# Seven products instead of eight in more weight units of the down projections of a transformer block, and a wider spacing of such units in the output projections

## The chip, the core and the metric

The kernel runs on one core of a Trainium2 chip. The metric is the device time in microseconds of one execution. A core has a matrix engine (TensorE, PE in the profile, with its weight loads as PEld), VectorE (DVE), ScalarE (ACT), GpSimd (POOL) and SyncE (SP), which here starts nearly all transfers. Each engine takes its instructions in program order, and they wait for each other by semaphores.

## What is computed

One layer of a streaming encoder block in float32: 256 tokens, width D = 2048, a feed-forward width of 5632, 256 memory tokens.

```python
def swiglu(h, w_gate, w_up, w_down):
    return (jax.nn.silu(h @ w_gate) * (h @ w_up)) @ w_down

def reference(...):
    x = x + 0.5 * swiglu(rms_norm(x, ffn1_norm), ffn1_w_gate, ffn1_w_up, ffn1_w_down)
    h = rms_norm(x, mix_norm)
    u, q, k, v, g, a_lr = split(h @ w_in)          # one combined projection
    y = concatenate([pool_mixer(u, ...), gla_mixer(q, k, v, g, a_lr, ...)])
    x = x + y @ w_out
    x = x + mem_cross_attention(rms_norm(x, xattn_norm), rms_norm(mem, mem_norm), w_q, w_kv, w_o)
    x = x + 0.5 * swiglu(rms_norm(x, ffn2_norm), ffn2_w_gate, ffn2_w_up, ffn2_w_down)
    return rms_norm(x, final_norm)
```

## The kernel before

**Units.** All weights (some 418 MB are read from HBM) pass through the core once, in pieces of 1 MB, called units: a raw tile of 128x2048 float32, of which three are held. Two units ahead of its use (`AHEAD = 2`), a unit is split for products in fp32r: ACT copies the raw tile to its high part `wh` (L247), DVE subtracts to get the low part `wl` (L248); `wh` and `wl` have three buffers each. A product in float32 is then three matmuls, high by high, high by low and low by high (`products`, L325 to L330), each with a 128x128 tile of activations as the stationary operand and 512 columns of weights passing by. What goes between units (evictions, splits of activations, sums) is given to the stream as `st.op(f, n)`: after n more units. ACT's and DVE's order is held to the order of the program around the weights by `in_turn` and `among_weights`.

**Plain and seven.** A unit of a down or an output projection holds two k tiles of 128 and two column groups of 512 for both halves of 128 tokens: 8 products, 24 matmuls (L330). A unit "by sevens" (`seven`, matmuls in L456) does the same 2x2x2 block with Winograd's form of Strassen's scheme: 7 products, 21 matmuls. For that DVE forms sums T of the weight's quarters (L431), ACT and DVE split T (`wh` in L434, `wl` in L435) and three quarters of the raw tile (`xh` in L247, `xl` in L248). `Sums.make` forms the sums of the activations of one pair of k tiles, and writes over half of that pair in `ys`, so that from then on only units by sevens can read it. The scope of the output projections gives T and `xh` one pair of buffers to share and `xl` a single one.

**A block.** `block_s` multiplies into 1024 columns of x. The four whole products P2, P4, P3, P0 take two PSUM tiles of two banks; the parts P1, P6, P7, P5, which the units by sevens alone need, take two more. The pool has four such tiles in all. After the last unit by sevens, `combine` adds the parts up (ACT copy L512, DVE L513, L514, L517) and `merge` adds the two sums to x early (L707); at the block's end the residual adds the whole products (DVE, L695). A block without sevens is `block_t`.

**Who adds into x.** `into_x` does an output or a down projection as two halves of 1024 columns, for w_out, w_o and five of the six downs. Each feed-forward network is cut into three parts (`FF_PARTS`): two whole downs of 16 k tiles (8 units per half) and a rest of 12 k tiles (6 units per half). The second network's rest has a block of its own, `down_end`, and isn't touched here. Before, the whole downs and the output projections have pair 0 by sevens in the first half and pairs 0 and 4 in the second; the rest of the first network runs as `block_t`, without sevens.

**What follows the rest of the first network.** Each half of its result is folded: PE transposes 512 columns of x into one PSUM tile (`px`, L718), ACT and DVE split it into `xs` (L216, L217) for the next projection, and ACT takes the squares of x (L729). After the second half, the row factor of the norm is formed (an activation table load and a root on ACT, L195, and small steps on DVE), and w_in begins (`pa` tiles, L315). w_in's first two units of a block need the columns of the first half alone, its third and fourth those of the second.

The changed kernel's lines from `block_s` on are shifted: L454 for L456, L516 to L521 for L512 to L517, L699 for L695, L711 for L707, L722 for L718, L733 for L729.

Of the kernel before, what the change touches and what calls it, by code (L numbers as in the profile page):

```python
# [18 lines left out]
FF = 5632  # L19
# [71 lines left out]
def build(ctx, tc, I, out):  # L91
# [146 lines left out]
    def among_weights(f):  # L238


        scalar, vector = behind_weights(f)
        latest["vector"] = vector
        if scalar is not None:
            latest["scalar"] = scalar
# [127 lines left out]
    class Sums:  # L372
# [3 lines left out]
        def __init__(self, name, act, pairs, over):  # L376
            self.name, self.act, self.pairs, self.over = name, act, pairs, over
# [59 lines left out]
        ))  # L437
        return [[x.rearrange("p (b n) -> p b n", n=NB) for x in (th, tl, rh, rl)]], None

    def seven(banks, act, sums, g, fresh, ends, weights):  # L440
        th, tl, rh, rl = weights
        k0, k1, lo, hi = 2 * g, 2 * g + 1, slice(0, P), slice(P, S)
        a11, a12, a22 = ([act[:, k, p, t] for p in range(2)] for k, t in ((k0, lo), (k1, lo), (k1, hi)))
        s3, n1, n4, s2 = sums.parts(g)
        table = {
            "P1": (a11, rh[:, 0], rl[:, 0]), "P3": (n4, rh[:, 1], rl[:, 1]),
            "P2": (a12, rh[:, 2], rl[:, 2]), "P5": (n1, th[:, 0], tl[:, 0]),
            "P7": (s3, th[:, 1], tl[:, 1]), "P6": (s2, th[:, 2], tl[:, 2]),
            "P4": (a22, th[:, 3], tl[:, 3]),
        }  # L450
        order = ("P1", "P7", "P5", "P6", "P2", "P3", "P4") if "P1" in fresh else (
            "P1", "P2", "P3", "P7", "P5", "P6", "P4")
        for n in order:
            (a, b), wh, wl = table[n]  # L454
            for j, (x, w) in enumerate(((a, wh), (a, wl), (b, wh))):
                nc.tensor.matmul(  # L456
                    banks[n], x, w, start=n in fresh and j == 0, stop=n in ends and j == 2
                )

    def block_s(srcs, act, sums, order, evict, merge=None, sevens=None, late=0):  # L460

        sevens = [g for g in order if g in (sevens or sums.pairs)]
        held, seen = {"banks": {}}, set()

        def banks(*names):
            t = ptile(uid("pt"))
            for i, n in enumerate(names):
                held["banks"][n] = t[:, i]  # L470
            return t

        def open_whole():
            if "ps" not in held:
                c = banks("P2", "P4")
                held["ps"] = (banks("P3", "P0"), c)

        def open_parts():
            held["parts"] = (banks("P1", "P6"), banks("P7", "P5"))

        names = {(1, 0): "P2", (1, 1): "P4", (0, 0): "P3", (0, 1): "P0"}

        def unit_s(g):
            def fn(weights):
                if g == sevens[0]:
                    open_parts()
                open_whole()
                fresh = {f"P{i}" for i in range(1, 8)} - seen
                seen.update(fresh)
                ends = ("P1", "P5", "P6", "P7") if g == sevens[-1] else ()  # L490
                seven(held["banks"], act, sums, g, fresh, ends, weights)
            return fn

        def unit_p(g):
            def fn(wh, wl):
                open_whole()
                wh, wl = (w.rearrange("p (k j n) -> p k j n", j=2, n=NB) for w in (wh, wl))
                for j in (1, 0):
                    for h in range(2):
                        n = names[j, h]  # L500
                        for kk in range(2):
                            products(held["banks"][n], act, 2 * g + kk, h, wh[:, kk, j],
                                     wl[:, kk, j], n not in seen and kk == 0,
                                     g == order[-1] and kk == 1)
                        seen.add(n)
            return fn

        def combine():

            e = held["e"] = scope["pool"].tile([P, 4, NB], F32, tag="sg", name=uid("sg"), bufs=2)  # L510
            a, b = held["parts"]
            nc.scalar.copy(e[:, 0], a[:, 0])  # L512
            nc.vector.tensor_tensor(out=e[:, 3], in0=a[:, 1], in1=e[:, 0], op=ALU.add)  # L513
            nc.vector.tensor_tensor(  # L514
                out=e[:, 1:3], in0=b, in1=e[:, 3:4].to_broadcast([P, 2, NB]), op=ALU.add
            )  # L516
            last = nc.vector.tensor_tensor(out=e[:, 3], in0=b[:, 1], in1=e[:, 1], op=ALU.add)  # L517
            if merge is not None:
                merge(e[:, 2:4], e[:, 0:2])
            return None, last  # L520

        def join(j):
            if merge is not None:
                evict(j, held["ps"][j])
                return
            e = held["e"][:, 0:2] if j else held["e"][:, 2:4]
            among_weights(lambda: (None, nc.vector.tensor_tensor(  # L527
                out=e, in0=held["ps"][j], in1=e, op=ALU.add if j else ALU.subtract
            )))
            evict(j, e)  # L530

        for g in order:
            if g in sevens:
                st.unit(srcs[g], unit_s(g), split_seven)
                if g == sevens[-1]:
                    st.op(combine if merge else lambda: among_weights(combine), late)
            else:
                st.unit(srcs[g], unit_p(g))
        for j in (1, 0):
            st.op(lambda j=j: join(j))  # L540
# [150 lines left out]
    def residual(scale, b, last=1):  # L691

        def evict(j, ps):
            x = x_cols((2 * b + j) * NB, NB)
            nc.vector.scalar_tensor_tensor(  # L695
                out=x, in0=ps, scalar=scale, in1=x, op0=ALU.mult, op1=ALU.add
            )
            if j == last:
                store_x(b)  # L699
        return evict  # L700

    def early_parts(scale, b):

        def merge(minus, plus):
            for j, e, s in ((1, plus, scale), (0, minus, -scale)):
                x = x_cols((2 * b + j) * NB, NB)
                nc.vector.scalar_tensor_tensor(  # L707
                    out=x, in0=e, scalar=s, in1=x, op0=ALU.mult, op1=ALU.add
                )
        return merge  # L710

    def fold(c, gain):
# [14 lines left out]
        for h in range(2):  # L727
            q = tmp.tile([P, NB], F32, tag="j", name=uid("j"))
            nc.scalar.activation(q, x[:, h], AF.Square, accum_out=ss[:, h, c : c + 1])  # L729


    Y_PAIRS, Y_ORDER, Y_SEVEN = (0, 4), ((1, 2, 3, 4, 0, 5, 6, 7), (1, 2, 0, 3, 4, 5, 6, 7)), ((0,), (0, 4))
    y_sums = Sums("ye", ys, Y_PAIRS, True)  # L733

    def make_y_sums(first=2):
        for g, after in zip(Y_PAIRS, (first, 4)):
            st.op(lambda g=g: among_weights(lambda: y_sums.make(g)), after)

    def into_x(w, act, scale, gain=None, k0=0, nk=KT, spread_too=True, src=None,
               sums=None):  # L740

        for b in range(2):
            st.op(lambda b=b: fetch_x(b, src), 2)
            cols = wwide(w, b * 2 * NB, k0, nk)
            if sums is None:
                block_t(cols, act, residual(scale, b))
            else:
                block_s(cols, act, sums, Y_ORDER[b], residual(scale, b, 0), early_parts(scale, b),
                        Y_SEVEN[b])
            if gain is not None:  # L750
                for j in range(2):
                    st.op(lambda c=2 * b + j: fold(c, gain), 1)
        if gain is not None:
            st.op(lambda: finish_norm(4, spread_too), 2)
            if spread_too:
                st.op(spread_norm, 3)
# [7 lines left out]
    def ffn(wg, wu, wd, down, amid=None):  # L764
# [40 lines left out]
        for lo, n in FF_PARTS:  # L805
# [18 lines left out]
            if n % 2:  # L824
# [5 lines left out]
                        ev_up(0, c)  # L830
                block_s(wtwo(wu, wg, (lo + n - 1) * NB), xs, x_sums, ORDER, both)
                st.op(lambda n=n: turn(gate[0], 4 * (n - 1)), 1)
            if whole:
                make_y_sums()
            down(wd, 4 * lo, 4 * n, lo + n == FF // NB, y_sums if whole else None)

    st.op(lambda: spare_transposes(12))
    st.op(lambda: turn_gains(0, G_MIX))
# [11 lines left out]
    st.op(more_gains, 14)  # L850
    st.op(lambda: turn_gains(G_MIX, G_END), 35)

    def down_first(wd, k0, nk, last, sums):
        into_x(wd, ys, 0.5, G_MIX if last else None, k0, nk, src=None if k0 else I["x"][0],
               sums=sums)

    ffn(I["ffn1_w_gate"][0], I["ffn1_w_up"][0], I["ffn1_w_down"][0], down_first,
        amid_first)
# [321 lines left out]
        for j in range(4):  # L1180
            split_scaled(xs, 4 * c + j, v[:, j, :], gcol(G_MEM + 4 * c + j))

    make_y_sums(1)
    into_x(I["w_out"][0], ys, 1.0, G_X, sums=y_sums)
    st.op(mem_in, 2)
    for c in range(4):
        st.op(lambda c=c: behind_weights(lambda: mem_squares(2 * c, 2 * c + 2)), c + 3)
# [75 lines left out]
    for h in range(H):  # L1263
# [2 lines left out]
        st.op(lambda h=h: probs(h), 3)  # L1266
        block_b(wblock(w_kv, D + h * NB), xs, ev_V)
        st.op(lambda h=h: values(h), 1)
    make_y_sums(0)
    into_x(w_o, ys, 1.0, G_FFN2, spread_too=False, sums=y_sums)  # L1270
    st.op(close_scope, 1)
    st.op(open_scope("s_ffn2"), 1)

# [4 lines left out]
        fin["gB"] = scope["pool"].tile([P, D], F32, tag="T", name="gB")  # L1278
        nc.sync.dma_start(fin["gB"], I["final_norm"].partition_broadcast(P))

    def down_last(wd, k0, nk, last, sums):
        if last:
            down_end(wd, k0, nk)
        else:
            into_x(wd, ys, 0.5, None, k0, nk, sums=sums)

    def down_end(wd, k0, nk):

# [193 lines left out]
```

## Time and profile before

| | |
|---|---|
| time, median of 3 runs | 2101.9 us (2101.67 to 2102.31) |
| profiled execution: its own time | 2101.99 us |
| profiled execution: span of its instructions | 2100.2 us |
| mean granted TensorE clock | 0.998 |
| PE busy | 2085.5 us (99%), 9916 matmuls |
| DVE busy | 1704.1 us (81%) |
| ACT busy | 1108.3 us (53%) |
| DMA | 435.95 MB, mean 208 GB/s |

The span goes from the first to the last instruction of the profiled execution; its own time is somewhat longer. A row of the timeline or of a group names the engine, the line of the kernel, the operation, `out<-in` by the names of the tiles (without buffer numbers) and the shape; in brackets stands how long the engine had been idle before it and what ended that. Matmuls are pipelined: one that is listed with 0.39 us can be followed by the next after 0.23.

### The profile page before, as it was taken

To read this page: it belongs to the slowest core of one execution; us is meant where nothing else is said; L and a number is where in the kernel's file an instruction comes from. 1 tells how busy PE (TensorE), PEld (TensorE's weight loads), DVE (VectorE), ACT (ScalarE), POOL (GpSimd) and SP (SyncE) were. 2 spreads that over 40 slices of the span, in tenths; PEclk is the share of its full clock that TensorE was granted. 3 is DMA by queue.
4 is the path that set the end of the run, shared out by engine and by line. 5 is a ranking of instruction groups with operands and counts; after the bars stand their busy time and mean duration, and the time that the engine had idled before them with its cause. 6 is when DMAs were issued, how large, how long until landed. Compare 5 with 4: busy or idle time off the path is not lost.

```text
span 2100.2 us, 24513 instructions
## 1 busy us (share of the span) xinstructions
PE 2085.5 (99%) x9916; PEld 1743.5 (83%) x9916; DVE 1704.1 (81%) x1537; ACT 1108.3 (53%) x1084; POOL 14.1 (1%) x41
## 2 busy tenths in 40 slices
PE   9999999999999999999999999999999999999998
PEld 7878888888888888888888888888888888888886
DVE  7998899988996677688765555779998999989974
ACT  7654455644554555364645444466554556545544
POOL 0000000000000000000000000000000000000001
PEclk9999999999999999999999999999999999999999
DMA  7656666566656555467755555656577665676673
GB/s 262 202 198 221 239 220 210 190 238 234 210 198 254 195 180 195 152 195 246 253 180 166 172 165 168 213 198 223 181 238 226 226 202 189 222 243 216 206 257 118
DMA packets 143610, 435.95 MB, mean 208 GB/s; under 512 B 9861, under 2 KB 13545, under 8 KB 143113
## 3 DMA queue, kind: packets, MB, share of 16 engines
q1 hardware_dynamic: 143464, 434.38, 61.4%
q8 instruction: 78, 1.28, 0.2%
q14 instruction: 36, 0.29, 0.0%
q10 hardware_dynamic: 32, 0.01, 0.0%
HBM read 417.58 MB, written 16.78 MB: 207 GB/s over the span
## 4 chain that ended last, share of the span: by engine, by line
PE 93%; DVE 4%; issue 1%; ACT 1%; DMA 0%; SPq 0%; DVEq 0%
PE pt L330 45%; PE pt L456 20%; PE pa L315 15%; PE pb L330 6%; PE pe L330 3%; DVE T L431 1%; PE ph L797 1%; DVE wl L248 1%; DVE wl L435 1%; DVE xl L248 1%; PE pl L1217 1%; PE pv L1252 1%; PE px L718 0%; ACT wh L247 0%; DVE sg L527 0%
## 5 line engine op out<-in xcount | busy, mean ns | idle before, releaser
L248 DVE TENSOR_TENSOR wl<-raw,wh 128x2048 fp32r<-128x2048 f32 (+2 forms) x284 | 637.9, 2251 | 268.4 <-ACT wh L247 267.3
L247 ACT CAST wh<-raw 128x2048 fp32r<-128x2048 f32 (+2 forms) x284 | 533.1, 1881 | 396.5 <-PE pt L330 170.1
L330 PE MATMUL pt<-wh,xs 128*128 128x512 f32 x1536 | 494.8, 390 | 0.4 <-ACT xs L216 0.4
L330 PE MATMUL pt<-wh,ys 128*128 128x512 f32 x1440 | 449.0, 390 | 0.0
L434 ACT CAST wh<-T 128x1024 fp32r<-128x1024 f32 x196 | 206.0, 1053 | 307.2 <-DVE T L431 281.1
L330 PEld LDWEIGHTS pt<-wh,xs 128*128 128x128 f32 x1536 | 287.5, 188 | 59.5 <-ACT xs L216 0.6
L330 PEld LDWEIGHTS pt<-wh,ys 128*128 128x128 f32 x1440 | 269.9, 188 | 56.0 <-ACT wh L247 0.4
L315 PE MATMUL pa<-xs,wh 128*128 128x512 f32 x896 | 315.9, 397 | 0.0
L330 PE MATMUL pt<-wl,xs 128*128 128x512 f32 x768 | 299.8, 390 | 0.0
L330 PE MATMUL pt<-wl,ys 128*128 128x512 f32 x720 | 280.5, 390 | 0.0
L315 PE MATMUL pa<-xs,wl 128*128 128x256 f32 x896 | 248.3, 281 | 0.0
L435 DVE TENSOR_TENSOR wl<-T,wh 128x2048 fp32r<-128x2048 f32 x98 | 223.9, 2285 | 1.5 <-ACT wh L434 1.3
L315 PEld LDWEIGHTS pa<-xs,wh 128*128 128x128 f32 x896 | 167.6, 188 | 38.1 <-issue 0.3
L248 DVE TENSOR_TENSOR xl<-raw,xh 128x1536 fp32r<-128x1536 f32 x98 | 171.7, 1752 | 12.9 <-ACT xh L247 12.9
L315 PEld LDWEIGHTS pa<-xs,wl 128*128 128x128 f32 x896 | 169.1, 189 | 1.7 <-issue 0.2
L330 PEld LDWEIGHTS pt<-wl,xs 128*128 128x128 f32 x768 | 144.2, 188 | 30.0 <-DVE wl L248 0.2
L330 PEld LDWEIGHTS pt<-wl,ys 128*128 128x128 f32 x720 | 135.2, 188 | 28.0
L247 ACT CAST xh<-raw 128x1536 fp32r<-128x1536 f32 x98 | 145.0, 1479 | 21.9 <-PE pt L456 16.5
L431 DVE TENSOR_TENSOR T<-T,raw 128x512 f32<-128x512 f32 x196 | 135.4, 691 | 5.6
L456 PE MATMUL pt<-wh,xs 128*128 128x512 f32 x320 | 124.6, 389 | 0.0
L456 PE MATMUL pt<-wh,xe 128*128 128x512 f32 x320 | 123.9, 389 | 0.0
L456 PE MATMUL pt<-xh,xs 128*128 128x512 f32 x320 | 120.0, 392 | 1.7 <-DVE sg L527 1.6
(236 smaller groups left out, 2341.7 us busy)
## 6 DMA issues: line engine op xcount, KB each, us to landing
raw<-in_ffn_w_down SPq DMA_DIRECT2D x88, 1024.0 KB, 5.4
raw<-in_ffn_w_up SPq DMA_DIRECT2D x80, 1024.0 KB, 5.0
raw<-in_ffn_w_gate SPq DMA_DIRECT2D x77, 1024.0 KB, 5.0
raw<-in_w_in SPq DMA_DIRECT2D x32, 1024.0 KB, 5.2
raw<-in_xattn_w_kv SPq DMA_DIRECT2D x32, 1024.0 KB, 5.3
raw<-in_w_out SPq DMA_DIRECT2D x16, 1024.0 KB, 5.6
raw<-in_xattn_w_q SPq DMA_DIRECT2D x16, 1024.0 KB, 6.0
raw<-in_xattn_w_o SPq DMA_DIRECT2D x16, 1024.0 KB, 5.6
```

The lines of the kernel that those rows point to most:

```text
L247: in_turn("scalar", lambda: nc.scalar.copy(hi, src))
L248: in_turn("vector", lambda: nc.vector.tensor_tensor(out=lo, in0=src, in1=f32(hi), op=ALU.subtract))
L315: nc.tensor.matmul(o, w, x, start=k == 0 and i == 0, stop=last and i == 1)
L330: nc.tensor.matmul(ps, a, w, start=first and i == 0, stop=last and i == 2)
L431: in_turn("vector", lambda: nc.vector.tensor_tensor(out=o, in0=a, in1=b, op=ALU.add))
L434: in_turn("scalar", lambda: nc.scalar.copy(th[:, c], t[:, c]))
L435: in_turn("vector", lambda: nc.vector.tensor_tensor(out=tl, in0=t, in1=f32(th), op=ALU.subtract))
L456: nc.tensor.matmul(banks[n], x, w, start=n in fresh and j == 0, stop=n in ends and j == 2)
L797: nc.tensor.transpose(v[:, i, h * P : (h + 1) * P], g[:, h, i * P : (i + 1) * P], ident)
L1217: nc.tensor.matmul(ps[:, t, :M], ys[:, 4 * h + d, a, tok], xa["K"][:, d, b, :], start=i == 0, stop=i == 11,)
L1252: nc.tensor.matmul(ps[:, d, :S], xa["V"][:, m, a, col], xa["PT"][:, m, b, :], start=i == 0, stop=i == 5,)
```

## The change

Where units by sevens stand, and how many there are, is now given for each kind of projection by a small class `IntoX`: pairs, when the sums of activations are made, the order of the units in both halves, and which pairs run by sevens.

- Whole downs (`WHOLE`): pairs 0 and 4 by sevens in both halves, where the first half had only pair 0; pair 4 moves to the seventh place of the first half, and its sums are made a unit later.
- Output projections (`OUTPUT`): the same pairs as before; in the second half two plain units stand between the two by sevens, where there was one.
- The last down of the first network (`REST`): pair 0 by sevens in the first half, pairs 0 and 2 in the second, three units in all, through `block_s` and with sums of the activations, where it had none.
- The order of the seven products in a unit that is not its block's first one by sevens becomes P1, P2, P4, P3, P5, P6, P7 (was P1, P2, P3, P7, P5, P6, P4) in these projections.

```diff
+                if "P1" in fresh:
+                    order = ("P1", "P7", "P5", "P6", "P2", "P3", "P4")
+                elif merge:
+                    order = ("P1", "P2", "P4", "P3", "P5", "P6", "P7")
+                else:
+                    order = ("P1", "P2", "P3", "P7", "P5", "P6", "P4")
...
-    Y_PAIRS, Y_ORDER, Y_SEVEN = (0, 4), ((1, 2, 3, 4, 0, 5, 6, 7), (1, 2, 0, 3, 4, 5, 6, 7)), ((0,), (0, 4))
-    y_sums = Sums("ye", ys, Y_PAIRS, True)
-
-    def make_y_sums(first=2):
-        for g, after in zip(Y_PAIRS, (first, 4)):
-            st.op(lambda g=g: among_weights(lambda: y_sums.make(g)), after)
...
+    class IntoX:
+        def __init__(self, pairs, after, orders, sevens):
+            self.sums = Sums("ye", ys, pairs, True)
+            self.after, self.orders, self.sevens = after, orders, sevens
+
+        def make_sums(self, after=None):
+            for g, n in zip(self.sums.pairs, after or self.after):
+                st.op(lambda g=g: among_weights(lambda: self.sums.make(g)), n)
+
+    WHOLE = IntoX((0, 4), (2, 5), ((1, 2, 3, 5, 0, 6, 4, 7), (1, 2, 0, 3, 4, 5, 6, 7)),
+                  ((0, 4), (0, 4)))
+    OUTPUT = IntoX((0, 4), (0, 4), ((1, 2, 3, 4, 0, 5, 6, 7), (1, 2, 0, 3, 5, 4, 6, 7)),
+                   ((0,), (0, 4)))
+    REST = IntoX((0, 2), (2, 4), ((1, 2, 3, 4, 0, 5), (1, 3, 0, 4, 2, 5)), ((0,), (0, 2)))
...
-            if sums is None:
-                block_t(cols, act, residual(scale, b))
-            else:
-                block_s(cols, act, sums, Y_ORDER[b], residual(scale, b, 0), early_parts(scale, b),
-                        Y_SEVEN[b])
+            block_s(cols, act, way.sums, way.orders[b], residual(scale, b, 0),
+                    early_parts(scale, b), way.sevens[b])
...
-            if whole:
-                make_y_sums()
-            down(wd, 4 * lo, 4 * n, lo + n == FF // NB, y_sums if whole else None)
+            down(wd, 4 * lo, 4 * n, lo + n == FF // NB, WHOLE if whole else REST)
...
-    make_y_sums(1)
-    into_x(I["w_out"][0], ys, 1.0, G_X, sums=y_sums)
+    OUTPUT.make_sums((1, 4))
+    into_x(I["w_out"][0], ys, 1.0, G_X)
...
-    make_y_sums(0)
-    into_x(w_o, ys, 1.0, G_FFN2, spread_too=False, sums=y_sums)
+    OUTPUT.make_sums()
+    into_x(w_o, ys, 1.0, G_FFN2, spread_too=False)
```

More of the change, by code (lines that the diff above doesn't have):

```diff
@@ L438, in split_seven, with seven @@
         return [[x.rearrange("p (b n) -> p b n", n=NB) for x in (th, tl, rh, rl)]], None
-    def seven(banks, act, sums, g, fresh, ends, weights):
+    def seven(banks, act, sums, g, fresh, ends, weights, order):
         th, tl, rh, rl = weights
@@ L450, in seven @@
         }
-        order = ("P1", "P7", "P5", "P6", "P2", "P3", "P4") if "P1" in fresh else (
-            "P1", "P2", "P3", "P7", "P5", "P6", "P4")
         for n in order:
@@ L490, in fn @@
                 ends = ("P1", "P5", "P6", "P7") if g == sevens[-1] else ()
-                seven(held["banks"], act, sums, g, fresh, ends, weights)
+                if "P1" in fresh:
[4 more added lines that the diff above has]
+                    order = ("P1", "P2", "P3", "P7", "P5", "P6", "P4")
+                seven(held["banks"], act, sums, g, fresh, ends, weights, order)
             return fn
@@ L729, in fold, with into_x @@
             nc.scalar.activation(q, x[:, h], AF.Square, accum_out=ss[:, h, c : c + 1])
-    Y_PAIRS, Y_ORDER, Y_SEVEN = (0, 4), ((1, 2, 3, 4, 0, 5, 6, 7), (1, 2, 0, 3, 4, 5, 6, 7)), ((0,), (0, 4))
-    y_sums = Sums("ye", ys, Y_PAIRS, True)
-    def make_y_sums(first=2):
-        for g, after in zip(Y_PAIRS, (first, 4)):
-            st.op(lambda g=g: among_weights(lambda: y_sums.make(g)), after)
-    def into_x(w, act, scale, gain=None, k0=0, nk=KT, spread_too=True, src=None,
-               sums=None):
+    class IntoX:
[10 more added lines that the diff above has]
+    REST = IntoX((0, 2), (2, 4), ((1, 2, 3, 4, 0, 5), (1, 3, 0, 4, 2, 5)), ((0,), (0, 2)))
+    def into_x(w, act, scale, gain=None, k0=0, nk=KT, spread_too=True, src=None, way=OUTPUT):
         for b in range(2):
@@ L851, in build, with down_first @@
     st.op(lambda: turn_gains(G_MIX, G_END), 35)
-    def down_first(wd, k0, nk, last, sums):
+    def down_first(wd, k0, nk, last, way):
+        way.make_sums()
         into_x(wd, ys, 0.5, G_MIX if last else None, k0, nk, src=None if k0 else I["x"][0],
-               sums=sums)
+               way=way)
     ffn(I["ffn1_w_gate"][0], I["ffn1_w_up"][0], I["ffn1_w_down"][0], down_first,
@@ L1279, in last_gain, with down_last @@
         nc.sync.dma_start(fin["gB"], I["final_norm"].partition_broadcast(P))
-    def down_last(wd, k0, nk, last, sums):
+    def down_last(wd, k0, nk, last, way):
         if last:
@@ L1284, in down_last @@
         else:
-            into_x(wd, ys, 0.5, None, k0, nk, sums=sums)
+            way.make_sums()
+            into_x(wd, ys, 0.5, None, k0, nk, way=way)
     def down_end(wd, k0, nk):
```

## The prediction

> **What bounds the kernel now.** I read the busy times and the slices first, then the list of what TensorE waited for, then the chain that ended last.
>
> ```profile
> PE 2085.5 (99%) x9916; PEld 1743.5 (83%) x9916; DVE 1704.1 (81%) x1537; ACT 1108.3 (53%) x1084; POOL 14.1 (1%) x41
> ...
> PEclk9999999999999999999999999999999999999999
> ```
>
> TensorE (PE) is busy 2085.5 of 2100.2 us, at full clock in every slice. A product removed is therefore time removed, as long as its operands still come in time. VectorE (DVE) at 81% is the engine whose queue can be late.
>
> ```profile
> PE pt L456 <- DVE sg L527: 1.6, 4, 1.0
> PE pwarm L186 <- POOL ident masks.py:199: 1.4, 1, 1.4
> PE px L654 <- DMA x<-in_x: 0.9, 1, 0.9
> PE pt L456 <- DVE xl L248: 0.7, 2, 0.3
> ```
>
> Columns: total wait in us, how often, the longest. There is almost nothing to win from waits (the four rows make 4.6 us), and much to lose: any new wait of PE counts in full, because no later wait could swallow it.
>
> ```profile
> 204.35 4.76 PE pt L456 x21
> 209.11 27.20 PE pt L330 x120
> ```
>
> These two pieces of the chain (start, us, line, count) lie in the first whole down. 27.20/120 = 4.76/21 = 0.2267 us per 128x512 product in both kinds of unit: a plain 1 MB unit of 24 products takes 5.44 us of PE, one by seven products (21) takes 4.76.
>
> **The change, part by part.** All against the profiled execution (2101.99 us; its span 2100.2 and 1.8 around it), which lies 0.09 above the median 2101.9.
>
> *Products.* Each of the four whole downs takes one more unit by sevens (pair 4 in the first half), the last down of the first network takes three: 7 x 3 = 21 products less. 21 x 0.2267 = **-4.76 us**, if PE waits for nothing new.
>
> *Output products.* In the second half of w_out and w_o the two units by sevens have one plain unit between them; they get two.
>
> ```profile
> 980.45 1.48 ACT L247 CAST xh<-raw 128x1536 fp32r<-128x1536 f32 x1 [5.41 <-PE pt L456]
> ...
> 981.96 1.76 DVE L248 TENSOR_TENSOR xl<-raw,xh 128x1536 fp32r<-128x1536 f32 x1 [6.41 <-ACT xh L247]
> ...
> 982.97 0.46 PE L456 MATMUL pt<-wh,ys 128*128 128x512 f32 x1
> 983.77 0.50 PE L456 MATMUL pt<-xl,ys 128*128 128x512 f32 x1 [0.34 <-DVE xl L248]
> ...
> 986.54 0.39 PE L456 MATMUL pt<-wh,ys 128*128 128x512 f32 x1
> ...
> 1368.94 0.46 PE L456 MATMUL pt<-wh,ys 128*128 128x512 f32 x1
> 1369.74 0.50 PE L456 MATMUL pt<-xl,ys 128*128 128x512 f32 x1 [0.34 <-DVE xl L248]
> ```
>
> Timeline rows: start, us, engine, line, and in brackets the idle time before with its end. ACT's copy xh of the second such unit waits 5.41 us until PE has read out the first one's; xl follows it on DVE, and PE arrives before xl is done. From 982.97 to 986.54 there are 11 products: 3.57 - 11 x 0.2267 = 1.08 us lost, and at 1368.94 the same wait stands again. The plain unit put between moves PE's need back by 5.44 us; the 1.08 of lateness and the 2.29 of that unit's own subtraction (the row at 253.25, below) leave 2.1 us. So both waits go: **-2.1 us**. Bounds: 0 (the copy is still late) and -2.2.
>
> *Whole downs.* In the first half the second seven now stands one plain unit before the half's end, so the combine of its parts (four DVE steps and two merges into x) meets the residual and the next unit's preparation at the boundary. The same steps stood in the trace already in the second half, in this order:
>
> ```profile
> 251.25 0.69 DVE L513 TENSOR_TENSOR sg<-pt,sg 128x512 f32<-128x512 f32 x1 [0.42 <-ACT sg L512]
> 251.97 1.23 DVE L514 TENSOR_TENSOR sg<-pt,sg 128x1024 f32<-128x1024 f32 x1
> 253.25 2.29 DVE L248 TENSOR_TENSOR wl<-raw,wh 128x2048 fp32r<-128x2048 f32 x1
> 255.46 1.22 DVE L431 TENSOR_TENSOR T<-raw 128x1024 f32<-128x1024 f32 x1
> 256.60 0.68 DVE L517 TENSOR_TENSOR sg<-pt,sg 128x512 f32<-128x512 f32 x1
> 257.20 1.22 DVE L707 SCALAR_TENSOR_TENSOR x<-sg,x 128x1024 f32<-128x1024 f32 x1
> 258.33 0.69 DVE L431 TENSOR_TENSOR T<-T,raw 128x512 f32<-128x512 f32 x1
> 258.93 1.22 DVE L707 SCALAR_TENSOR_TENSOR x<-sg,x 128x1024 f32<-128x1024 f32 x1
> 260.07 0.68 DVE L431 TENSOR_TENSOR T<-T,raw 128x512 f32<-128x512 f32 x1
> 260.67 1.75 DVE L248 TENSOR_TENSOR xl<-raw,xh 128x1536 fp32r<-128x1536 f32 x1
> 262.34 2.28 DVE L435 TENSOR_TENSOR wl<-T,wh 128x2048 fp32r<-128x2048 f32 x1
> ```
>
> Count from the end of part P6 (after it ACT's copy of 0.6 us). By the start-to-start steps of these rows DVE takes 0.72 + 1.28 (sums of parts) + 2.21 (wl of the next plain unit) + 1.14 (T) + 0.60 + 1.13 (merge) + 0.60 (T) + 1.14 (merge) + 1.13 (residual, priced as a merge, same shape) + 0.60 (T) + 1.67 (xl) + 1.13 (residual) + 2.29 (wl of T): 0.66 + 15.64 = 16.3 us. PE has 76 products to issue between P6's last and the first that reads this wl: 76 x 0.2267 = 17.2, less 0.16 by which a product ends after its slot (0.39 against 0.2267): 17.07. **The margin is about 0.75 us**, at four places; the next plain units' wl have 1.0 to 1.2. So I cost it at nothing, with DVE's queue as the thin cover. If DVE comes x us later than this, each place costs x - 0.75. No transfer is moved by more than a unit, and none is near its need.
>
> *Last down of the first network.* Here PE waited for nothing before. In the changed program's queues three things follow from the two buffers of PSUM that the fold of x's first half holds: the parts P1, P5, P6, P7 of both sevens of the second half can't begin until DVE has split the folded columns, and their 24 products stand at the very end of the down. Until then those two units (128 and 130) keep two of the three wh and wl buffers.
>
> ```profile
> 690.54 1.91 ACT L247 CAST wh<-raw 128x2048 fp32r<-128x2048 f32 x1
> ...
> 692.49 2.29 DVE L248 TENSOR_TENSOR wl<-raw,wh 128x2048 fp32r<-128x2048 f32 x1 [1.45 <-ACT wh L247]
> ...
> 711.02 2.51 DVE L695 SCALAR_TENSOR_TENSOR x<-pt,x 128x1024 f32<-128x1024 f32 x2
> ...
> 712.10 0.39 PE L315 MATMUL pa<-xs,wh 128*128 128x512 f32 x1
> ...
> 714.12 0.62 ACT L729 ACTIVATE j<-x 128x512 f32<-128x512 f32 x1
> ...
> 727.68 4.50 DVE L248 TENSOR_TENSOR wl<-raw,wh 128x2048 fp32r<-128x2048 f32 x2 [1.31 <-ACT wh L247]
> ...
> 731.74 0.28 PE L315 MATMUL pa<-xs,wl 128*128 128x256 f32 x1
> ```
>
> (a) Unit 131 has only the buffer of 129. Its cast can start when 129's last product has ended; cast and subtraction take 4.24 us (690.54 to 694.78), with the 0.2 of product end and semaphore 4.45. PE has 11 products ahead of the first that needs the wl (nine of seven 130 and the first of 131, by the queue): 2.49. New wait **2.0 us**.
> (b) The first tile of w_in takes the PSUM buffer of P1 and P6, which is free when DVE's first sum of parts has read it. In DVE's queue the wl of unit 133 stands ahead of that sum, and its cast waits for unit 128's buffer, read last 12 products before the down's end. 0.2 + 1.95 (cast) + 2.2 (wl) + 0.69 (sum) - 12 x 0.2267 = **2.3 us**.
> (c) The residual is now behind everything. From the last product's slot DVE does that sum (start at 1.62, 0.60), a wl (2.20), the sums (1.28, 0.60), two merges (1.13 each) and two residuals (1.13, 1.22): 10.9 us. In the trace it was done 1.4 us after (711.02 + 2.51 against 712.10). Squares, rsqrt, the splits of the folded columns 2 and 3 and the wl of w_in's fourth unit hang on it. Before, the squares began 2.0 us after w_in's first product (714.12, 712.10). Now w_in's first product comes 2.3 after the slot and the squares 10.9: 8.6, so the chain runs 6.6 us later against PE. The fourth unit's wl was done at 729.97 (727.68, and 2.29 for the first of the two) and needed at 731.74: 1.8 of cover. 6.6 - 1.8 = **4.8 us**, split over waits for the third unit's xs (about 1.5) and the fourth's wh and wl (the rest).
> Sum of (a) to (c): **+9.1 us**. Bounds: 4.3 if the chain of (c) is hidden whole (the trace hid 1.8 of it, no row hides more); 12 if, besides, the first half's buffers cost as (a) does and DVE loses another 1 us in (c). I take 9.1, since each step has a row of the same operation and shape.
>
> Sum: -4.76 - 2.1 + 0 + 9.1 = **+2.2 us: 2104.2 for the profiled execution, 2104.1 by the median**. About 0.2% (4.2 us) is what a measurement of this kernel tells from no change, so it comes out within that.
>
> **Rivals.**
> 1. *Faster: products count, waits don't come.* 2101.9 - 4.76 - 2.1 = 2095.0; with (a) and (b) alone 2099.3. For it: PE's share of 99% and only 4.6 us of waits in the whole trace, though DVE's queue held the same steps in other downs. Against: in the whole downs no fold holds PSUM, and there is no rsqrt behind the residual; here the queue order leaves PE nothing else to issue. 0.15.
> 2. *Slower: DVE is late at the boundary of the whole downs.* It decides from 0.75 us of lateness, at four places. With 1.5 us each costs 0.75: 3.0, 2107.0. For it: the margin is a sum of thirteen steps, and ACT and DVE hand xh, wh and T to each other there. Against: in the rows above these steps ran back to back. 0.10.
> 3. *The output products' wait stays* (the change doesn't do what it says): the xh buffer is still asked for too early or the next unit's xh takes the wait. 2106.1. Against: 2.1 us of spare. 0.07.
> 4. *The last down costs more:* its first half, with a seven and the combine there, loses what (a) loses, and (c) 1 us more: 2107.0 to 2108. 0.08.
> 5. *The clock falls.* This row is the last 10.2 us of the span (columns: busy us and count of PE, PEld, DVE, ACT, POOL; then the granted clock):
>
> ```profile
> 2090.00:2100.20 10.20, 0.59 (x3) 0.17 (x1) 3.94 (x11) 3.38 (x9) 0.99 (x1) 0.66 0.56 202
> ```
>
> With PE nearly idle the clock granted is 0.66 there. The waits of (b) and (c) come within 25 us of each other; if they brought one such stretch, 0.34 x 10.20 = 3.5 us more: 2107.5. Against: none of them is longer than about 2.3 us, and the waits listed at the head (1.4 us the longest) were passed at full clock. 0.05.
> The Trainium skill (TensorE: Matmul & The Clock Gate, "The HAM clock gate" and "HAM oscillation") says that the array's clock halves after an idle window of some 3.4 us, and warns of PE gaps longer than that. By that rule a wait of 2.3 us alone leaves the clock, and the sum stays; the last row's 0.66 agrees with a fall after a few us of idleness, and no run here shows the threshold.
> The skill speaks for (a) and (b) too: Trainium Kernel Development and Optimization, "Best Practices", says that consistent bubbles can mean that SBUF or PSUM ran out.
>
> **How the numbers follow.** The forecast has 0.55; its own range, with 7 to 11 us for the last down, is 2102 to 2106. Rival 1 lies below 2097.7 with 0.12 and above it with 0.03. Of the rest, rivals 2, 4 and 5 are over 2106.1 with 0.20 together, rival 3 with half of its 0.07, and the forecast's upper edge with 0.03. That makes faster 0.12, same 0.61, slower 0.27. The range of 8 in 10 goes from 2098.5 (most of rival 1 outside) to 2108.
>
> **What would show it.** Right: in the changed kernel's waits of PE, the rows for xl at 983 and 1370 are gone; about 2 us appear in the second half of the last down for wh and wl; then, in the 30 us after it, 2.3 for the sum of parts and 4 to 5 for xs and wh; the residual ends some 11 us after the down's last product; the whole downs are 0.68 us shorter each with no wait. Wrong: no PE wait between 690 and 740 (rival 1), waits for T's wl in the whole downs (rival 2), or a granted clock under 1 after the last down (rival 5).

## The result and the profile after

The changed kernel takes 2107.74 us (median of 8 runs, 2106.69 to 2108.51) against 2101.99 (8 runs, 2101.32 to 2102.38): 5.75 us slower, ratio 1.0027, 95% interval 1.0016 to 1.0038. The profiled execution has 2108.27 us and a span of 2106.5, 6.3 more than before.

The first row of the profile's page, and then the waits of PE in the changed kernel (total us, times, longest):

```profile
PE 2085.8 (99%) x9895; PEld 1743.1 (83%) x9895; DVE 1743.9 (83%) x1589; ACT 1120.0 (53%) x1104; POOL 13.1 (1%) x41
```

```profile
PE pa L315 <- ACT wh L247: 2.6, 2, 1.6
PE pa L315 <- DVE sg L517: 2.2, 1, 2.2
PE pt L330 <- DVE wl L248: 2.2, 2, 1.1
PE pt L454 <- DVE sg L531: 1.6, 4, 1.0
PE pwarm L186 <- POOL ident masks.py:199: 1.4, 1, 1.4
PE pt L330 <- ACT wh L247: 0.4, 1, 0.4
```

PE has 21 matmuls less (the prediction calls each matmul of 128x512 a product, and so does this part) and is still busy for 0.3 us more. The rows for xl are gone, as forecast for the output projections. New are waits of `pa` (w_in) for the first sum of parts (2.2) and for wh (2.6), and of `pt` for wl (2.2) and wh (0.4): one wl of 1.1 in the last down, and one that was not forecast.

The timeline around the end of the last down, PE first, then DVE and ACT:

```profile
713.22 0.50 PE L315 MATMUL pa<-xs,wh 128*128 128x512 f32 x1 [2.21 <-DVE sg L517]
...
714.85 0.63 PE L315 MATMUL pa<-xs,wh 128*128 128x512 f32 x1
715.28 0.41 PE L315 MATMUL pa<-xs,wl 128*128 128x256 f32 x1
715.49 0.63 PE L315 MATMUL pa<-xs,wh 128*128 128x512 f32 x1
...
717.33 0.40 PE L315 MATMUL pa<-xs,wh 128*128 128x512 f32 x1
...
735.62 0.73 PE L315 MATMUL pa<-xs,wh 128*128 128x512 f32 x2 [1.55 <-ACT wh L247]
737.42 1.01 PE L315 MATMUL pa<-xs,wh 128*128 128x512 f32 x2 [1.07 <-ACT wh L247]
...
710.27 2.29 DVE L248 TENSOR_TENSOR wl<-raw,wh 128x2048 fp32r<-128x2048 f32 x1 [0.39 <-ACT wh L247]
712.48 0.68 DVE L517 TENSOR_TENSOR sg<-pt,sg 128x512 f32<-128x512 f32 x1
713.08 2.28 DVE L248 TENSOR_TENSOR wl<-raw,wh 128x2048 fp32r<-128x2048 f32 x1
...
719.41 2.35 DVE L699 SCALAR_TENSOR_TENSOR x<-pt,x 128x1024 f32<-128x1024 f32 x2
...
721.79 0.63 ACT L733 ACTIVATE j<-x 128x512 f32<-128x512 f32 x1 [8.85 <-DVE x L699]
```

The last product of the down has its slot at 710.62 to 710.85. PE then waits for DVE's first sum, which stands behind a wl (the rows at 710.27 and 712.48), as read from the queue. The residual ends at 721.76, 10.9 us after that slot (forecast 10.9), and the squares begin right behind.

What was not in the sum is between 713.8 and 717.2: a pair of products, wh and wl, takes 0.64 us (714.85 to 715.49) where it takes 0.35 elsewhere. The stretches of the changed kernel (busy us and count of PE, PEld, DVE, ACT, POOL; granted clock; DMA):

```profile
715.00:717.00 2.00, 2.00 (x8) 1.71 (x7) 1.97 (x3) 0.00 (x0) 0.00 (x0) 0.50 1.04 400
719.00:721.00 2.00, 2.00 (x13) 1.77 (x12) 2.00 (x3) 0.00 (x0) 0.32 (x1) 1.00 0.52 200
735.00:740.00 5.00, 3.32 (x11) 2.46 (x12) 4.41 (x2) 4.17 (x3) 0.00 (x0) 0.77 0.17 27
```

TensorE ran at half clock for some 3.4 us after the 2.2 us wait, and again from 737.7 to 741.1 after 1.55 and 1.07 (the ends are read from slices of half a microsecond). In 3.4 us at half clock PE does 1.7 us less of its work; how much of that reaches the time is told with the last down, below.

The stages, by the starts of their first and last products in the traces of both (us):

| stage | before | after | difference |
|---|---|---|---|
| four whole downs together | 346.3 | 343.6 | -2.7 |
| last down of the first network | 67.76 | 67.85 | +0.1 |
| from its end to w_out (w_in, pool, GLA) | 204.69 | 213.56 | +8.9 |
| w_out | 87.73 | 86.57 | -1.2 |
| from its end to w_o | 295.34 | 296.37 | +1.0 |
| w_o | 90.62 | 89.47 | -1.15 |
| from its end to the second network's first down | 170.48 | 171.80 | +1.3 |

They make +6.25, the whole difference of the spans. Each of the three parts of the change now has its own lines: the whole downs gained what was forecast, the output projections gained 2.3 and gave 2.3 back right behind, and the last down costs 9.0 net.

### The profile page after: what moved, and what is told of

Read it like the earlier page. It is cut to its first block, busy times and chain, and to the rows that moved or that the text cites. A ratio compares the mean times of both kernels' runs of the same rounds, so it can differ in the third digit from the quotient of the medians.

```text
span 2106.5 us, 24569 instructions
## 1 busy us (share of the span) xinstructions
PE 2085.8 (99%) x9895; PEld 1743.1 (83%) x9895; DVE 1743.9 (83%) x1589; ACT 1120.0 (53%) x1104; POOL 13.1 (1%) x41
## 4 chain that ended last, share of the span: by engine, by line
PE 90%; DVE 5%; ACT 2%; issue 2%; DMA 1%; SPq 0%; DVEq 0%; ACTq 0%
PE pt L330 42%; PE pt L454 21%; PE pa L315 14%; PE pb L330 6%; PE pe L330 3%; DVE wl L248 1%; ACT wh L247 1%; DVE T L431 1%; PE ph L807 1%; DVE wl L435 1%; DVE xl L248 1%; PE pl L1226 1%; PE pv L1261 1%; DMA raw<-in_xattn_w_q 0%; DVE xs L217 0%
## 5 line engine op out<-in xcount | busy, mean ns | idle before, releaser
L248 DVE TENSOR_TENSOR wl<-raw,wh 128x2048 fp32r<-128x2048 f32 (+2 forms) x277 | 621.4, 2249 | 219.2 <-ACT wh L247 218.4
L247 ACT CAST wh<-raw 128x2048 fp32r<-128x2048 f32 (+2 forms) x277 | 519.3, 1880 | 321.7 <-PE pt L330 88.6
L330 PE MATMUL pt<-wh,ys 128*128 128x512 f32 x1328 | 418.9, 390 | 0.4 <-ACT wh L247 0.4
L434 ACT CAST wh<-T 128x1024 fp32r<-128x1024 f32 x210 | 220.9, 1053 | 345.6 <-DVE T L431 336.8
L330 PEld LDWEIGHTS pt<-wh,ys 128*128 128x128 f32 x1328 | 248.9, 188 | 52.1 <-ACT wh L247 0.8
L330 PE MATMUL pt<-wl,ys 128*128 128x512 f32 x664 | 258.8, 390 | 1.1 <-DVE wl L248 1.1
L435 DVE TENSOR_TENSOR wl<-T,wh 128x2048 fp32r<-128x2048 f32 x105 | 239.8, 2283 | 1.6 <-ACT wh L434 1.3
L248 DVE TENSOR_TENSOR xl<-raw,xh 128x1536 fp32r<-128x1536 f32 x105 | 183.8, 1751 | 11.1 <-ACT xh L247 11.1
L330 PEld LDWEIGHTS pt<-wl,ys 128*128 128x128 f32 x664 | 124.7, 188 | 27.3 <-DVE wl L248 1.6
L431 DVE TENSOR_TENSOR T<-raw 128x1024 f32<-128x1024 f32 x105 | 127.8, 1217 | 0.5
```

Source lines behind the costliest of these rows:

```text
L247: in_turn("scalar", lambda: nc.scalar.copy(hi, src))
L248: in_turn("vector", lambda: nc.vector.tensor_tensor(out=lo, in0=src, in1=f32(hi), op=ALU.subtract))
L330: nc.tensor.matmul(ps, a, w, start=first and i == 0, stop=last and i == 2)
L431: in_turn("vector", lambda: nc.vector.tensor_tensor(out=o, in0=a, in1=b, op=ALU.add))
L434: in_turn("scalar", lambda: nc.scalar.copy(th[:, c], t[:, c]))
L435: in_turn("vector", lambda: nc.vector.tensor_tensor(out=tl, in0=t, in1=f32(th), op=ALU.subtract))
```

## The experiments

Each kernel stands against the kernel before on the same chip. The diffs show only the lines that place the units; a part that is undone gets its former order of the seven products back as well.

**One part at a time.** The whole downs alone (`WHOLE` as in the change; the other two as before):

```diff
-    OUTPUT = IntoX(..., ((1, 2, 3, 4, 0, 5, 6, 7), (1, 2, 0, 3, 5, 4, 6, 7)), ((0,), (0, 4)))
-    REST = IntoX((0, 2), ...)
+    OUTPUT = IntoX(..., ((1, 2, 3, 4, 0, 5, 6, 7), (1, 2, 0, 3, 4, 5, 6, 7)), ((0,), (0, 4)))
+    REST = None    # block_t
```

> The kernel before with the change of the whole downs alone (one more unit by sevens in the first half of each, four in all, 12 products less). My theory (the products count in full, since the combine at the half boundary just fits DVE's queue): 12 x 0.2267 = 2.7 us less, ratio 0.9987, and no PE wait in any of the four whole downs. Rival (DVE is late at the boundary): less than 1.5 us gained or a loss, with PE waits for wl of T or xl near the boundaries.

Measured: 2099.37 against 2101.49, ratio 0.9989 (0.9981 to 0.9998). The downs take 86.0, 85.9, 85.9 and 85.9 us in its trace, where the first two of before take 86.7 and 86.5; no wait of PE is new in them. From the first product of the first down to PE's last one it is 2.9 us shorter. The thin margin at the half boundary is in the trace (of the changed kernel, first whole down; ACT, DVE, PE):

```profile
221.38 0.59 ACT L516 COPY sg<-pt 128x512 f32<-128x512 f32 x1 [4.84 <-PE pt L454]
...
235.40 2.28 DVE L435 TENSOR_TENSOR wl<-T,wh 128x2048 fp32r<-128x2048 f32 x1
...
238.41 0.39 PE L454 MATMUL pt<-wl,ys 128*128 128x512 f32 x1
```

From ACT's copy to the end of wl are 16.3 us, as in the sum, and PE's first product that reads this wl starts 0.73 later. In the other three whole downs, and in all four of this kernel, it is the same within 0.01.

The output projections alone:

```diff
-    WHOLE = IntoX((0, 4), (2, 5), ((1, 2, 3, 5, 0, 6, 4, 7), ...), ((0, 4), (0, 4)))
-    REST = IntoX((0, 2), ...)
+    WHOLE = IntoX((0, 4), (2, 4), ((1, 2, 3, 4, 0, 5, 6, 7), ...), ((0,), (0, 4)))
+    REST = None    # block_t
```

> The kernel before with the wider spacing in w_out and w_o alone. Theory now, from the trace of the changed kernel: the two waits for xl go (-2.1 us), but combine and residual end one unit later, and the norm's factor, the splits of x and the weights of the next projection's fourth unit with them, so that PE waits about 0.7 us at the start of w_q and 1.3 at the start of the second network: sum -0.1, ratio 1.000. Rival, as forecast: no new wait, -2.1 us, ratio 0.999; the waits at w_q and the second network then come from the lateness that the last down leaves.

Measured: 2101.64 against 2101.49, ratio 1.0001 (0.9992 to 1.0010). In its trace w_out takes 86.57 and w_o 89.46 us, 1.16 less each, and the stages behind them take 1.0 and 1.3 more. The waits of PE no longer name xl, but have a new one, and it stands at the start of the second network:

```profile
PE pt L330 <- DVE wl L248: 1.0, 1, 1.0
```

At w_q the list has no wait of that size, but the first block of w_q ends 1.0 later after w_out. Nothing is late ahead in this kernel, so the lateness of the last down isn't the cause. The residual of w_o before, and that of the changed kernel with the wl it delays (DVE, then PE):

```profile
1389.40 2.51 DVE L695 SCALAR_TENSOR_TENSOR x<-pt,x 128x1024 f32<-128x1024 f32 x2
```

```profile
1395.02 2.28 DVE L248 TENSOR_TENSOR wl<-raw,wh 128x2048 fp32r<-128x2048 f32 x1
1397.22 2.35 DVE L699 SCALAR_TENSOR_TENSOR x<-pt,x 128x1024 f32<-128x1024 f32 x2
...
1414.23 2.29 DVE L248 TENSOR_TENSOR wl<-raw,wh 128x2048 fp32r<-128x2048 f32 x1 [1.31 <-ACT wh L247]
...
1416.58 0.50 PE L330 MATMUL pt<-wl,xs 128*128 128x512 f32 x1 [1.03 <-DVE wl L248]
```

Before, the residual ended 1.65 us after the start of the last product (1391.91 against 1390.26); after, 2.98 (1399.57 against 1396.59). With the second unit by sevens one place later, combine, merges and residual are closer together, and squares, root, splits and the next projection's fourth unit hang on the residual. PE came 1.2 us earlier to a chain that had not become earlier: from w_o's first product to the residual's end are 92.3 us before and 92.5 after.

In w_out another link is late. The second half of the residual stands behind a wl of w_q there, that wl behind ACT's cast, and the cast behind the transfer of w_q's second unit (ACT before; then the changed kernel: SyncE's longest wait there, ACT, DVE):

```profile
1001.03 1.92 ACT L247 CAST wh<-raw 128x2048 fp32r<-128x2048 f32 x1 [0.80 <-DMA raw<-in_xattn_w_q]
```

```profile
SPq L568 <- DVE xl L248: 10.4, 1, 10.4
```

```profile
1009.40 1.91 ACT L247 CAST wh<-raw 128x2048 fp32r<-128x2048 f32 x1 [6.96 <-DMA raw<-in_xattn_w_q]
...
1011.34 2.29 DVE L248 TENSOR_TENSOR wl<-raw,wh 128x2048 fp32r<-128x2048 f32 x1 [1.32 <-ACT wh L247]
1013.55 1.22 DVE L699 SCALAR_TENSOR_TENSOR x<-pt,x 128x1024 f32<-128x1024 f32 x1
```

SyncE starts the next transfer, w_q's first unit, when the xl of the second unit by sevens is done, and that is now later: from 990 to 996 nothing is transferred. The cast begins 1.35 us before w_out's last product (1009.40 against 1010.75), where it began 3.3 before it (1001.03 against 1004.30), and DVE sits idle for 1.32 us with half of the residual still to do.

The last down alone:

```diff
-    WHOLE = IntoX((0, 4), (2, 5), ..., ((0, 4), (0, 4)))
-    OUTPUT = IntoX(..., (1, 2, 0, 3, 5, 4, 6, 7)), ((0,), (0, 4)))
+    WHOLE = IntoX((0, 4), (2, 4), ..., ((0,), (0, 4)))
+    OUTPUT = IntoX(..., (1, 2, 0, 3, 4, 5, 6, 7)), ((0,), (0, 4)))
```

> The kernel before with the three units by sevens in the last down of the first network alone (9 products less). Theory: nearly all the loss is here: -2.0, then waits of 2.0 (one buffer left for wh and wl), 2.3 (first PSUM tile of w_in) and 4.8 less what PE's own slowness hides, and two stretches of half clock after the longer waits, 1.6 us each: +8 to +9, ratio 1.004. Rival: the loss is spread over the three parts of the change, and this one costs under 6.

Measured: 2112.73 against 2101.49, ratio 1.0051 (1.0038 to 1.0063). The profiled execution was the fastest of the five, 2110.69, and its clock is 1.00 through the whole stage:

```profile
710.00:715.00 5.00, 3.25 (x15) 2.36 (x13) 4.61 (x3) 4.21 (x3) 0.00 (x0) 1.00 0.33 76
715.00:720.00 5.00, 4.54 (x25) 3.97 (x26) 4.97 (x5) 0.19 (x1) 0.00 (x0) 1.00 1.02 382
```

So it shows the three waits by themselves, as they are at full clock. The down takes 67.86 us, 0.1 more in spite of 2.04 less work: (a) is 2.1. From the down's last product to w_in's first are 2.60 us (712.86 to 715.46) where there were 0.22: (b) is 2.4. From there to w_out it is 209.37 against 204.47: (c) is 4.9, of which 1.3 are lost up to the end of w_in's third unit and 3.6 at the fourth. Together 9.4, less 2.04: 7.4, and that is what its trace is longer from the first down on; 0.9 more lie ahead of that, in the first load of x. But its median is 2 us above this execution, hence the repeat:

> The same kernel as rest_only once more, for another profiled execution. In that of rest_only the granted clock stayed at 1.00 and the forecast waits alone stood there (7.4 us net), though the median was 11.2 above the kernel before. If executions differ by stretches of half clock after the longer waits, a slower execution shows a granted clock under 1 between 710 and 745 us and 0.997 or less on the whole; if not, the clock is 1.00 there again and the difference lies elsewhere.

Measured: 2112.58 against 2101.67, ratio 1.0051 (1.0037 to 1.0065); the profiled span is 2111.6, with a mean clock of 0.996. The stretches:

```profile
715.00:720.00 5.00, 4.93 (x19) 4.27 (x20) 4.97 (x5) 0.00 (x0) 0.00 (x0) 0.66 1.02 377
...
740.00:745.00 5.00, 4.47 (x14) 3.80 (x15) 5.00 (x3) 2.27 (x2) 0.00 (x0) 0.50 0.53 169
```

The same kernel with the same waits; in this execution, the slowest of its four, the clock fell twice, and w_in to w_out takes 213.0 us, 3.6 more than in the other. Stretches of half clock follow these waits in one execution and not in the other; kernels without the waits show none there. The mean clocks of all nine executions of this kernel agree: the two with 0.999 took 2110.6 and 2110.7 us, the seven with 0.996 or 0.997 took 2111.6 to 2113.7. All eight of the changed kernel have 0.997 or 0.998. What decides whether the clock falls isn't shown.

Alone, the three parts make -2.1 + 0.15 + 11.2 = +9.3, together 5.75. The first two together make -2.65 (below), which their intervals allow; the last down costs 9.0 in the trace of the changed kernel and 11.0 in this one, both with two stretches of half clock. These 2 us can be read from ACT's queue. In the changed kernel the root stands ahead of the first split of the folded columns. Alone it stands behind it, and that split waits for PE's transposes, which the first stretch of half clock has made later (changed kernel, then this one):

```profile
724.80 1.28 ACT L195 ACT_TABLE_LOAD   x1
...
726.75 0.47 ACT L216 ACTIVATE xs<-px,gains 128x256 fp32r<-128x256 f32 x1 [0.45 <-PE px L722]
```

```profile
728.88 0.47 ACT L216 ACTIVATE xs<-px,gains 128x256 fp32r<-128x256 f32 x1 [2.26 <-PE px L722]
729.37 1.28 ACT L195 ACT_TABLE_LOAD   x1
```

ACT's cast for w_in's fourth unit begins 24.3 us after the start of the down's last product here, 23.0 at full clock, and 23.05 in the changed kernel: there the first stretch is hidden, because PE waits for this cast at full clock too. That is 1.3 of the 2 us. The other 0.8 are in the second stretch, which lasts from 738.9 to 745.7 here, twice as long. The code of the last down is the same in both; why the root's place in the queue differs isn't shown. The rest of the gap between 9.3 and 5.75 lies within the intervals, 2.6 us either way for the last down alone.

**Where the units by sevens stand.** In w_out and w_o, pair 0 one place earlier in place of pair 4 one place later:

```diff
-    OUTPUT = IntoX(..., ((1, 2, 3, 4, 0, 5, 6, 7), (1, 2, 0, 3, 5, 4, 6, 7)), ((0,), (0, 4)))
+    OUTPUT = IntoX(..., ((1, 2, 3, 4, 0, 5, 6, 7), (1, 0, 2, 3, 4, 5, 6, 7)), ((0,), (0, 4)))
```

> The kernel before with another spacing in the second half of w_out and w_o: pair 0 one place earlier (1, 0, 2, 3, 4, 5, 6, 7) in place of pair 4 one place later. There are two plain units between the sevens, and combine stays where it was. If distance in units is what the wait for xl needs, both waits go with no new one behind: -2.1 us, ratio 0.999. If the parts P1, P5, P6, P7 of pair 0 can't begin before the fold of the first half has given its two PSUM tiles back, pair 0's products end at the same place as before and the wait for xl stays: 0 to -0.4 us, ratio 1.000.

Measured: 2101.86 against 2101.49, ratio 1.0001 (0.9993 to 1.0010). The wait stays, though there are two plain units between the two by sevens (ACT of this kernel, then PE):

```profile
979.55 1.48 ACT L247 CAST xh<-raw 128x1536 fp32r<-128x1536 f32 x1 [5.71 <-PE pt L454]
```

```profile
1368.86 0.50 PE L454 MATMUL pt<-xl,ys 128*128 128x512 f32 x1 [0.35 <-DVE xl L248]
```

Distance in the list of units isn't what counts. By the program's queue the products of the first unit's parts stand behind the fold, wherever that unit is, and hold its xh until then: in the trace that unit's first products start at 964.20, the last ones at 978.67, and ACT's copy waits for these. The order of the seven products is the new one in this kernel, so it isn't what removes the wait either. The queue is also what put the parts last in the last down.

In the last down, the second half's units by sevens two places earlier:

```diff
-    REST = IntoX((0, 2), (2, 4), ((1, 2, 3, 4, 0, 5), (1, 3, 0, 4, 2, 5)), ((0,), (0, 2)))
+    REST = IntoX((0, 2), (2, 4), ((1, 2, 3, 4, 0, 5), (1, 0, 2, 3, 4, 5)), ((0,), (0, 2)))
```

> The kernel before with three units by sevens in the last down, as in the change, but in the second half pairs 0 and 2 stand at places 2 and 3 (order 1, 0, 2, 3, 4, 5). By the queue the parts still follow the fold, and until then the two units hold two of the three wh and wl buffers, but two plain units follow the parts. If the loss at w_in comes from the parts being last (its first PSUM tile, the late residual), those waits go and no stretch of half clock stands there; what stays is the wait for the one buffer left and for xh, xl and T at the half boundary, some 5 to 6 us in pieces of at most 1.5. Sum -2.0 + 5.7: +3.7 us, ratio 1.0018. Rival (the units by sevens cost DVE too much in this down wherever they stand, and make the residual late): again +7 or more.

Measured: 2107.56 against 2101.67, ratio 1.0029 (1.0018 to 1.0039), +5.9. The waits at w_in are gone: from the down's end to w_out it takes 204.5 us, as before. The down itself takes 73.35, 5.6 more and 7.6 with the products saved: waits of 1.35 for x, 1.03 for xl, 0.85 for wh and 1.24 for wl at the half boundary, and then half clock again (PE of this kernel):

```profile
685.78 1.97 PE L722 MATMUL px<-ident,x 128*128 128x128 f32 x16 [1.35 <-DVE x L699]
688.77 0.50 PE L454 MATMUL pt<-xl,ys 128*128 128x512 f32 x1 [1.03 <-DVE xl L248]
...
691.05 0.50 PE L330 MATMUL pt<-wh,ys 128*128 128x512 f32 x1 [0.85 <-ACT wh L247]
...
693.77 0.80 PE L330 MATMUL pt<-wl,ys 128*128 128x512 f32 x1 [1.24 <-DVE wl L248]
694.36 1.05 PE L330 MATMUL pt<-wh,ys 128*128 128x512 f32 x2
```

The theory held for w_in; the price at the boundary was read as 5.7 and is the 7.6, of which the half clock from 693.7 to 697.2 takes 1.7. Moving the units trades one set of waits for another; neither of the two orders tried in six units is without them.

**Undoing it, and a better version.** The change without the units by sevens in the last down:

```diff
-    REST = IntoX((0, 2), (2, 4), ((1, 2, 3, 4, 0, 5), (1, 3, 0, 4, 2, 5)), ((0,), (0, 2)))
+    REST = None    # block_t
```

> The changed kernel without the units by sevens in the last down of the first network (whole downs and output spacing kept). If the parts add up: -2.7 for the whole downs, 0 for the spacing: -2.7 us, ratio 0.9987. Rival (the spacing pays once nothing is late before it): -4.8, ratio 0.9977.

Measured: 2099.02 against 2101.67, ratio 0.9988 (0.9979 to 0.9997): -2.65, where the whole downs alone gave -2.1 with an interval as wide. In its trace the spacing gains 0.45 (w_q costs 0.5 more in place of 1.0), which the times can't tell from nothing. The rival's -4.8 lies outside the interval.

> Whole downs as in the change, output projections as before, and in the last down of the first network pair 0 by sevens in the first half alone, with sums that leave the activations whole, so that the second half runs plain and no parts meet the fold. Products: 12 + 3 less, 15 x 0.2267 = 3.4 us, with no new wait: ratio 0.9984. If the first half's seven brings a wait at the boundary: -2.7 or less.

```diff
-    OUTPUT = IntoX(..., ((1, 2, 3, 4, 0, 5, 6, 7), (1, 2, 0, 3, 5, 4, 6, 7)), ((0,), (0, 4)))
-    REST = IntoX((0, 2), (2, 4), ((1, 2, 3, 4, 0, 5), (1, 3, 0, 4, 2, 5)), ((0,), (0, 2)))
+    OUTPUT = IntoX(..., ((1, 2, 3, 4, 0, 5, 6, 7), (1, 2, 0, 3, 4, 5, 6, 7)), ((0,), (0, 4)))
+    REST = IntoX((0,), (2,), ((1, 2, 3, 4, 0, 5), None), ((0,), ()), over=False)  # 2nd half block_t
```

Measured: 2098.41 against 2101.67, ratio 0.9985 (0.9976 to 0.9994): -3.3, of 3.4 in products. The last down takes 67.07 us, 0.69 less than before, and what follows 204.7, as before. It has the lowest median of all versions, below both kernels; its interval overlaps with those of the whole downs alone and of the version above.

## Why the prediction was right or wrong

The time lies inside the range and on the slower side of the forecast: +2.2 was forecast for the profiled execution, +6.3 came. The range of 8 in 10 (2098.5 to 2108) holds 2107.74, but the forecast's own range of 2102 to 2106 does not, and 0.27% is more than the 0.2% within which the change was to stay.

**Products, -4.76: right.** The whole downs gave 2.7 of it, the last down's share shows in (a) as the work that its waits replaced.

**Whole downs at no cost: right.** The margin of 0.75 us at the half boundary is 0.72 or 0.73 in all four places; rival 2 fell.

**Last down, +9.1: right in size and mechanism.** (a) 2.1 against 2.0, (b) 2.4 against 2.3, (c) 4.9 against 4.8, as the execution with a full clock shows. The parts come last, the residual 10.9 us after the last product, and the fourth unit's wh and wl behind it. The split of (c) holds too at full clock: 1.3 at the third unit (forecast 1.5) and 3.6 at the fourth. In the changed kernel itself the three come with the half clock on top.

**Output products, -2.1: this step failed.** "So both waits go" was right, 1.16 us each by the stages. What I left out is what the step itself asked for: what is late next. I priced the chain from the residual over the root to the next projection's fourth unit for the last down, as (c), and not for w_out and w_o, where the same chain follows: with a unit moved one place later the residual of w_o ends when it did, while the last product comes earlier (2.98 us before the residual's end, from 1.65). In w_out a transfer for w_q came too late as well, against "none is near its need". That gave back 1.0 and 1.3. The bound that I gave, 0, is the result, but not for the reason named with it, a copy that is still late; rival 3, by which the wait stays, fell.

**The clock, 0.05 as a rival: it happened.** The argument against it was that no wait is longer than 2.3 us, and that waits of up to 1.4 had passed at full clock. In some executions the wait of 2.2 us was enough, and so were four of 0.85 to 1.35 within ten us. Its price was forecast as 3.5; net it was 3.6 between the two executions of the last down alone, and 1.6 in the changed kernel (6.5 for (c) and both stretches, against 4.9 for (c) by itself), where the first stretch is hidden. The prediction says that no later wait could swallow a new wait of PE; the first stretch was swallowed by the lateness that w_in's third and fourth units have anyway. That rival 5's 2107.5 lies so near the measured 2107.74 is luck: it has 3.5 for the clock and still counts the 2.1 of the output projections as won. The Trainium skill (TensorE: Matmul & The Clock Gate, "HAM oscillation") warns of PE gaps over some 3.4 us. Read as a threshold, by that rule the clock should have stayed; the trace doesn't agree, with 0.50 granted after a gap of 2.2. The same page of the Trainium skill ("The HAM clock gate") gives a window of some 3.4 us, and that agrees with how long the stretches of half clock lasted: 3.4 us each in the changed kernel (713.8 to 717.2, 737.7 to 741.1), and twice that from 738.9 to 745.7 in the second execution of the last down alone.

The misses are 2.1 at the output projections, 1.6 of the clock and 0.3 in the sizes of (a) to (c). They turn +2.2 into +6.2; measured were 6.3.

## What to carry to other kernels

Where the matrix engine is busy for 99%, work taken off it pays only if everything that it waits for next was early by as much: after pricing the wait that goes, follow the chain behind it to the next stage, at every place where that chain exists, transfers included. A unit whose results need PSUM that another step holds keeps its weight buffers as well, so that one full pool stalls another. Leave units with extra work for VectorE away from a boundary behind which a norm hangs, and count waits that come close together as a risk to the clock too.

## What the runs showed of the hardware that was not expected

TensorE's granted clock fell to 0.50 for about 3.4 us (once for 6.8) after a single wait of 2.2 us, and after waits of 1.35, 1.03, 0.85 and 1.24 us between 684 and 694 us with work between them. It is not the same in every execution: one kernel kept 1.00 through waits of 2.21, 1.95 and 1.07 us in one profiled execution and fell twice in another, which makes 3.6 us, more than the gain of the whole downs. A fall need not cost its 1.7 us: in the changed kernel one was hidden behind a wait that PE has at full clock too.
